# Softmax-minus-one-hot on one core: blocks of two rows per partition in three in-place f32 buffers, with a row maximum

## The chip, the core and the metric

The kernel runs on one core of a Trainium2 chip. The metric is the device time of one execution in microseconds (us). The chip's engines have short names: DVE is the vector engine, ACT the scalar engine, POOL the GpSimd engine, PE the tensor engine, SP the engine that here only issues loads. Sixteen DMA engines move data between HBM (the chip's main memory) and SBUF (the on-chip buffer of 128 partitions).

## The reference, cut to what matters

```python
batch, seq_len, vocab = 8, 1024, 8192            # 8192 rows of 8192 f32
logits_max = np.max(logits, axis=-1, keepdims=True)
exp_logits = np.exp(logits - logits_max)
softmax = exp_logits / np.sum(exp_logits, axis=-1, keepdims=True)
one_hot[batch_idx, seq_idx, labels] = 1.0
return (softmax - one_hot).astype(np.float32)
```

268.4 MB are read and 268.4 MB are written, whatever the kernel does. A tile of 128 rows is 4 MB; there are 64 of them. "Row" below means such a row of tiles: one matrix row on each of the 128 partitions.

## The kernel before

One tile per step, four f32 buffers, exp without a shift, a bf16 copy for the arithmetic, and one label transfer per tile:

```python
io_pool   = tc.tile_pool(name="io", bufs=4)            # f32, 128 x 8192
work_pool = tc.tile_pool(name="work", bufs=2)          # bf16
# ... cut: iota over the vocabulary, once
for ti in range(n_tiles):
    nc.sync.dma_start(out=logits_tile[:], in_=logits_nv[rs : rs + P, :])           # L47
    nc.gpsimd.dma_start(out=labels_tile[:], in_=labels_n[rs : rs + P, None])       # L50
    # ... cut: labels to f32
    nc.scalar.activation(out=exp_bf[:], in_=logits_tile[:], func=Exp,
                         bias=0.0, scale=1.0, accum_out=sum_f32[:])                # L61
    nc.vector.reciprocal(out=recip_sum[:], in_=sum_f32[:])
    nc.vector.tensor_scalar(out=ohts_bf, in0=iota_pv[:, :], scalar1=labels_f32[:],
                            scalar2=sum_f32[:], op0=is_equal, op1=mult)            # L74
    nc.vector.tensor_sub(out=exp_bf[:], in0=exp_bf[:], in1=ohts_bf)                # L83
    nc.vector.tensor_scalar_mul(out=logits_tile[:], in0=exp_bf[:],
                                scalar1=recip_sum[:])                              # L85
    nc.scalar.dma_start(out=out_nv[rs : rs + P, :], in_=logits_tile[:])            # L87
```

The softmax here doesn't subtract the row's maximum and nothing guards it: scores larger than these inputs give would overflow.

## Time and profile before

| | before |
|---|---|
| time, median of 3 runs | 1255.14 us |
| span of the profiled run | 1252.6 us |
| DVE, ACT busy | 58%, 36% |
| per tile, mid-run | 19.36 us |
| one 32 KB packet on its DMA engine | 1.213 us |
| idle of all DMA engines together | one stretch, 4.3 us, at the end |

The page of the kernel before starts with the span, the engines' busy time, the busy tenths of the DMA engines in 40 equal slices, and what they moved in each slice:

```profile
span 1252.6 us, 992 instructions
...
DVE 732.6 (58%) x320; ACT 457.0 (36%) x129; POOL 253.0 (20%) x69
...
DMA  9999999999999999999999999999999999999997
GB/s 400 421 435 434 433 428 430 433 436 433 435 430 432 431 433 433 434 434 432 429 432 435 431 434 433 431 432 432 434 433 434 433 429 432 432 434 435 434 433 311
```

The DMA engines are busy in every slice. Only the first two slices and the last move less than 425 GB/s. A transfer of 4 MB is 8 packets on each of 16 engines, so 128 transfers take 128 x 8 x 1.213 = 1242 us (the data packets of the trace add up to 1244 us per engine): nearly the whole span.

Next the costliest groups (line, engine, operation, operands, count | busy us, mean ns | idle before, and what ended it):

```profile
L61 ACT ACTIVATE exp_bf<-logits_tile 128x8192 bf16<-128x8192 f32 x64 | 449.8, 7029 | 771.3 <-DMA logits_tile<-in_logits_dram 757.8
...
L85 DVE TENSOR_SCALAR logits_tile<-exp_bf,recip_sum 128x8192 f32<-128x8192 bf16 x64 | 287.1, 4486 | 0.1
L83 DVE TENSOR_TENSOR exp_bf<-exp_bf,logits_tile 128x8192 bf16<-128x8192 bf16 x64 | 283.2, 4425 | 2.2
L74 DVE TENSOR_SCALAR logits_tile<-iota_pv,labels_f,sum_f 128x8192 bf16<-128x8192 int16 x64 | 154.3, 2412 | 0.3 <-issue 0.3
```

DVE's three passes cost 4.49 + 4.43 + 2.41 us per tile. The waits, of the compute engines and of the load queue (us in total, times, longest):

```profile
ACT exp_bf L61 <- DMA logits_tile<-in_logits_dram: 757.8, 62, 19.2
DVE recip_sum L71 <- ACT exp_bf L61: 485.1, 61, 10.5
```

```profile
SPq L47 <- DMA out_dram<-logits_tile: 1169.6, 60, 50.2
```

ACT waits for loads, and loads wait for stores to free a buffer. The loop is closed by the DMA engines. At the very end nothing is left to overlap with. The timeline of the last tile (start, duration, what, idle before it):

```profile
1221.87 7.03 ACT L61 ACTIVATE exp_bf<-logits_tile 128x8192 bf16<-128x8192 f32 x1 [12.24 <-DMA logits_tile<-in_logits_dram]
1221.92 0.34 ACTq L87 DMA_DIRECT2D out_dram<-logits_tile  x1
...
1229.11 2.41 DVE L74 TENSOR_SCALAR logits_tile<-iota_pv,labels_f,sum_f 128x8192 bf16<-128x8192 int16 x1
1231.56 4.43 DVE L83 TENSOR_TENSOR exp_bf<-exp_bf,logits_tile 128x8192 bf16<-128x8192 bf16 x1
1236.02 4.49 DVE L85 TENSOR_SCALAR logits_tile<-exp_bf,recip_sum 128x8192 f32<-128x8192 bf16 x1
1240.54 0.34 ACTq L87 DMA_DIRECT2D out_dram<-logits_tile  x1
```

The last load landed just before 1221.87, the last store left at 1240.54. The store before it left at 1221.92 and was done in between.

### The profile page before, as it was taken

The page shows a single profiled execution, that of the slowest core. Times are in us where ns is not written, and L with a number is a line of the kernel's source. Part 1 is how long each engine was busy: PE and PEld are TensorE (multiplying, and loading weights), DVE is VectorE, ACT ScalarE, POOL GpSimd, SP SyncE. Part 2 cuts the span into 40 slices and gives each one's busy share as a digit, 9 for nine tenths or more (in the row PEclk, how much of TensorE's full clock was granted, in tenths as well). Part 3 has the DMA queues.
Part 4 walks back from the last instruction along what each step waited for, and adds up shares of the span by engine and source line. Part 5 has one row for each costly group of instructions (what it writes and reads, how often), then busy time and mean ns, then how long its engine had stood idle before and what let it go on. Part 6 is the DMA issues. An engine that isn't in the chain of part 4 may idle for free.

```text
span 1252.6 us, 992 instructions
## 1 busy us (share of the span) xinstructions
DVE 732.6 (58%) x320; ACT 457.0 (36%) x129; POOL 253.0 (20%) x69
## 2 busy tenths in 40 slices
DVE  3764655746647556465574664755646556465573
ACT  4424244243342433423424334243342432423422
POOL 5322212212122122221221212212222122100000
DMA  9999999999999999999999999999999999999997
GB/s 400 421 435 434 433 428 430 433 436 433 435 430 432 431 433 433 434 434 432 429 432 435 431 434 433 431 432 432 434 433 434 433 429 432 432 434 435 434 433 311
DMA packets 20487, 537.01 MB, mean 429 GB/s; under 512 B 4096, under 2 KB 4096, under 8 KB 4096
## 3 DMA queue, kind: packets, MB, share of 16 engines
q1 hardware_dynamic: 9216, 268.44, 49.8%
q10 hardware_dynamic: 9216, 268.44, 49.6%
q0 software_dynamic: 2048, 0.07, 0.1%
q14 instruction: 7, 0.06, 0.0%
HBM read 268.50 MB, written 268.44 MB: 429 GB/s over the span
## 4 chain that ended last, share of the span: by engine, by line
DMA 71%; DVE 17%; issue 8%; ACT 1%; POOL 1%; ACTq 0%; SPq 0%; PEldq 0%
DMA out_dram<-logits_tile 38%; DMA logits_tile<-in_logits_dram 32%; DVE logits_tile L85 7%; DVE exp_bf L83 7%; DVE logits_tile L74 4%; ACT exp_bf L61 1%; DMA labels_tile<-in_labels_dram 1%; POOL iota_pv L41 1%; ACTq L87 0%; POOL labels_tile L50 0%; DVE labels_f L57 0%; DVE recip_sum L71 0%; SPq L47 0%; ACTq L61 0%; PEldq L113 0%
## 5 line engine op out<-in xcount | busy, mean ns | idle before, releaser
L61 ACT ACTIVATE exp_bf<-logits_tile 128x8192 bf16<-128x8192 f32 x64 | 449.8, 7029 | 771.3 <-DMA logits_tile<-in_logits_dram 757.8
L50 POOL DMA_DIRECT2D labels_tile<-in_labels_dram x64 | 245.9, 3843 | 832.1 <-DVE labels_f L57 830.1
L71 DVE RECIPROCAL recip_sum<-sum_f 128x1 f32<-128x1 f32 x64 | 10.5, 163 | 485.1 <-ACT exp_bf L61 485.1
L85 DVE TENSOR_SCALAR logits_tile<-exp_bf,recip_sum 128x8192 f32<-128x8192 bf16 x64 | 287.1, 4486 | 0.1
L83 DVE TENSOR_TENSOR exp_bf<-exp_bf,logits_tile 128x8192 bf16<-128x8192 bf16 x64 | 283.2, 4425 | 2.2
L74 DVE TENSOR_SCALAR logits_tile<-iota_pv,labels_f,sum_f 128x8192 bf16<-128x8192 int16 x64 | 154.3, 2412 | 0.3 <-issue 0.3
L57 DVE CAST labels_f<-labels_tile 128x1 f32<-128x1 int32 x64 | 9.4, 147 | 20.2 <-DMA labels_tile<-in_labels_dram 20.2
L61 ACT ACTIVATION_READ_ACCUMULATOR exp_bf<-logits_tile 128x1 f32 x64 | 11.9, 186 | 0.0
L41 POOL IOTA iota_pv<- 128x8192 int16 x1 | 6.9, 6944 | 0.4 <-PEq L113 0.4
L61 ACT ACT_TABLE_LOAD x1 | 1.3, 1283 | 0.7 <-PEq L102 0.7
L102 POOL MEMSET const-float32-0.0<- 128x1 f32 x1 | 0.1, 99 | 0.2 <-issue 0.2
L102 POOL MEMSET const-bfloat16-1.0<- 128x1 bf16 x1 | 0.1, 102 | 0.0
L102 POOL MEMSET const-uint8-127<- 128x1 uint8 x1 | 0.1, 102 | 0.0
L102 POOL MEMSET const-float32-1.0<- 128x1 f32 x1 | 0.1, 99 | 0.0
## 6 DMA issues: line engine op xcount, KB each, us to landing
logits_tile<-in_logits_dram SPq DMA_DIRECT2D x64, 4096.0 KB, 27.2
out_dram<-logits_tile ACTq DMA_DIRECT2D x64, 4096.0 KB, 31.3
labels_tile<-in_labels_dram POOLq DMA_DIRECT2D x64, 1.0 KB, 12.7
```

What stands on the lines that cost most here:

```text
L41: nc.gpsimd.iota(iota_pv[:, :], [[1, V]], channel_multiplier=0)
L50: nc.gpsimd.dma_start(out=labels_tile[:], in_=labels_n[rs : rs + P, None])
L57: nc.vector.tensor_copy(out=labels_f32[:], in_=labels_i32)
L61: nc.scalar.activation(out=exp_bf[:], in_=logits_tile[:], func=mybir.ActivationFunctionType.Exp, bias=0.0, scale=1.0, accum_out=sum_f32[:],)
L71: nc.vector.reciprocal(out=recip_sum[:], in_=sum_f32[:])
L74: nc.vector.tensor_scalar(out=ohts_bf, in0=iota_pv[:, :], scalar1=labels_f32[:], scalar2=sum_f32[:], op0=mybir.AluOpType.is_equal, op1=myb ...
L83: nc.vector.tensor_sub(out=exp_bf[:], in0=exp_bf[:], in1=ohts_bf)
L85: nc.vector.tensor_scalar_mul(out=logits_tile[:], in0=exp_bf[:], scalar1=recip_sum[:])
L102: nc = _bacc.Bacc("TRN2", target_bir_lowering=False, num_devices=1)
```

## The change

The change loads two adjacent rows per partition as one contiguous run of 64 KB, works in place in f32 (no bf16 copy), and so fits three buffers of two rows where there were four of one. It adds the row maximum that the reference has. It loads all labels once and lays them out with two small transposes. The scaling moves from DVE to ACT. The instruction order is written by hand. The core of the diff (set-up, label code, tile allocations and `store` cut; `store` issues one transfer per row, from ACT, for the blocks in `BY_ROW_OUT`):

```diff
-    io_pool = ctx.enter_context(tc.tile_pool(name="io", bufs=4))
-    work_pool = ctx.enter_context(tc.tile_pool(name="work", bufs=2))
+    # SLOTS = 3, G = 2, HALF = 4096, C = V // HALF; T = 64 rows, B = 32 blocks
+    x_b = x_nv.rearrange("(b p j) v -> b p j v", p=P, j=G)
+    io = ctx.enter_context(tc.tile_pool(name="io", bufs=SLOTS))   # [P, G, V] f32
+    ctx.enter_context(tc.manual_schedule())
...
+    def load(b):            # L74 by row, L76 as a block
+        if b in BY_ROW_IN:
+            for j in range(G):
+                nc.sync.dma_start(out=x[:, j, :], in_=x_b[b, :, j, :])
         else:
+            nc.sync.dma_start(out=x[:], in_=x_b[b])
+    def row_max(x):         # L81
+        nc.vector.tensor_reduce(out=m[:], in_=x[:], axis=X, op=Alu.max, negate=True)
+    def exponent(x, m):     # L86
+        nc.scalar.activation(out=x[:], in_=x[:], func=Act.Exp, bias=m[:], accum_out=s[:])
+    def normalize(x, r):    # L97, two halves
+        nc.scalar.activation(out=xc, in_=xc, func=Act.Copy, bias=0.0, scale=r[:])
+    def subtract(t, x):     # L102, two halves
+        nc.vector.scalar_tensor_tensor(out=xc, in0=iota[:], scalar=lab[...], in1=xc,
+            op0=Alu.is_equal, op1=Alu.subtract, reverse1=True)
...
+    BY_ROW_IN = (0, B - 1)
+    BY_ROW_OUT = range(B)
+    m = row_max(row(0))
+    for t in range(T):
+        s = exponent(row(t), m)
+        r = inverse(s)
+        if t + 1 < T:
+            m = row_max(row(t + 1))
+        if t > 0:
+            store(t - 1)
+        normalize(row(t), r)
+        subtract(t, row(t))
+    store(T - 1)
```

More of the change, by code (lines that the diff above doesn't have):

```diff
@@ L5 @@
 import concourse.tile as tile
-from concourse import bass_utils, mybir
+from concourse import mybir
 from concourse._compat import with_exitstack
 P = 128
+HALF = 4096
+SLOTS = 3
+G = 2
 @with_exitstack
@@ L21 @@
     fp32 = mybir.dt.float32
-    bf16 = mybir.dt.bfloat16
+    i32 = mybir.dt.int32
     i16 = mybir.dt.int16
-    logits_nv = logits.flatten_outer_dims()
-    out_nv = out.flatten_outer_dims()
-    labels_n = labels
-    while len(labels_n.shape) > 1:
-        labels_n = labels_n.rearrange("a b ... -> (a b) ...")
-    N, V = logits_nv.shape
-    assert N % P == 0, f"N={N} must be a multiple of {P}"
-    n_tiles = N // P
-    const_pool = ctx.enter_context(tc.tile_pool(name="const", bufs=1))
-    io_pool = ctx.enter_context(tc.tile_pool(name="io", bufs=4))
@@ L37 @@
-    work_pool = ctx.enter_context(tc.tile_pool(name="work", bufs=2))
-    stats_pool = ctx.enter_context(tc.tile_pool(name="stats", bufs=4))
-    iota_pv = const_pool.tile([P, V], i16)
-    nc.gpsimd.iota(iota_pv[:, :], [[1, V]], channel_multiplier=0)
-    for ti in range(n_tiles):
-        rs = ti * P
-        logits_tile = io_pool.tile([P, V], fp32, tag="io")
-        nc.sync.dma_start(out=logits_tile[:], in_=logits_nv[rs : rs + P, :])
-        labels_tile = stats_pool.tile([P, 1], labels_n.dtype, tag="labels")
-        nc.gpsimd.dma_start(out=labels_tile[:], in_=labels_n[rs : rs + P, None])
-        labels_f32 = stats_pool.tile([P, 1], fp32, tag="labels_f32")
-        if mybir.dt.size(labels_n.dtype) == 8:
-            labels_i32 = labels_tile.bitcast(mybir.dt.int32)[:, :1]
-        else:
-            labels_i32 = labels_tile[:]
-        nc.vector.tensor_copy(out=labels_f32[:], in_=labels_i32)
-        exp_bf = work_pool.tile([P, V], bf16, tag="exp")
-        sum_f32 = stats_pool.tile([P, 1], fp32, tag="sum")
-        nc.scalar.activation(
-            out=exp_bf[:],
-            in_=logits_tile[:],
-            func=mybir.ActivationFunctionType.Exp,
-            bias=0.0,
-            scale=1.0,
-            accum_out=sum_f32[:],
-        )
-        recip_sum = stats_pool.tile([P, 1], fp32, tag="recip")
-        nc.vector.reciprocal(out=recip_sum[:], in_=sum_f32[:])
-        ohts_bf = logits_tile.bitcast(bf16)[:, :V]
-        nc.vector.tensor_scalar(
-            out=ohts_bf,
-            in0=iota_pv[:, :],
-            scalar1=labels_f32[:],
-            scalar2=sum_f32[:],
-            op0=mybir.AluOpType.is_equal,
-            op1=mybir.AluOpType.mult,
-        )
-        nc.vector.tensor_sub(out=exp_bf[:], in0=exp_bf[:], in1=ohts_bf)
-        nc.vector.tensor_scalar_mul(out=logits_tile[:], in0=exp_bf[:], scalar1=recip_sum[:])
-        nc.scalar.dma_start(out=out_nv[rs : rs + P, :], in_=logits_tile[:])
@@ new lines @@
+    Act = mybir.ActivationFunctionType
+    Alu = mybir.AluOpType
+    x_nv = logits.flatten_outer_dims()
+    o_nv = out.flatten_outer_dims()
+    N, V = x_nv.shape
+    T = N // P
+    B = T // G
+    C = V // HALF
+    lab_bp = labels.rearrange("a b -> (a b)").rearrange("(b q) -> b q", q=G * P)
+    x_b = x_nv.rearrange("(b p j) v -> b p j v", p=P, j=G)
+    o_b = o_nv.rearrange("(b p j) v -> b p j v", p=P, j=G)
+    const = ctx.enter_context(tc.tile_pool(name="const", bufs=1))
+    io = ctx.enter_context(tc.tile_pool(name="io", bufs=SLOTS))
@@ new lines @@
+    stats = ctx.enter_context(tc.tile_pool(name="stats", bufs=4))
+    psum = ctx.enter_context(tc.tile_pool(name="psum", bufs=1, space=bass.MemoryType.PSUM))
+    ctx.enter_context(tc.manual_schedule())
+    lab_raw = const.tile([B, G * P], labels.dtype)
+    nc.scalar.dma_start(out=lab_raw[:], in_=lab_bp)
+    iota = const.tile([P, HALF], i16)
+    nc.gpsimd.iota(iota[:], [[1, HALF]], base=0, channel_multiplier=0)
+    ident = const.tile([B, B], fp32)
+    nc.gpsimd.memset(ident[:], 0.0)
+    nc.gpsimd.affine_select(
+        out=ident[:], in_=ident[:], compare_op=Alu.not_equal, fill=1.0,
+        base=0, pattern=[[-1, B]], channel_multiplier=1,
+    )
@@ new lines @@
+    lab_f = const.tile([B, G, P], fp32)
+    step = mybir.dt.size(labels.dtype) // 4
+    lab32 = lab_raw[:].bitcast(i32).rearrange("b (p j s) -> b j p s", j=G, s=step)
+    lab = const.tile([P, C, G, B], fp32)
+    lab_ps = psum.tile([P, G, B], fp32)
+    for j in range(G):
+        nc.vector.tensor_copy(out=lab_f[:, j, :], in_=lab32[:, j, :, 0])
+        nc.tensor.transpose(out=lab_ps[:, j, :], in_=lab_f[:, j, :], identity=ident[:])
+    for c in range(C):
+        nc.vector.tensor_scalar_add(out=lab[:, c], in0=lab_ps[:], scalar1=float(-c * HALF))
@@ new lines, in load @@
+    def load(b):
+        x = io.tile([P, G, V], fp32, tag="x", name="x")
+        if b in BY_ROW_IN:
+            for j in range(G):
+                nc.sync.dma_start(out=x[:, j, :], in_=x_b[b, :, j, :])
+        else:
+            nc.sync.dma_start(out=x[:], in_=x_b[b])
+        return x
+    def row_max(x):
+        m = stats.tile([P, 1], fp32, tag="m", name="m")
+        nc.vector.tensor_reduce(out=m[:], in_=x[:], axis=mybir.AxisListType.X, op=Alu.max, negate=True)
+        return m
+    def exponent(x, m):
+        s = stats.tile([P, 1], fp32, tag="s", name="s")
+        nc.scalar.activation(out=x[:], in_=x[:], func=Act.Exp, bias=m[:], scale=1.0, accum_out=s[:])
+        return s
@@ new lines, in inverse @@
+    def inverse(s):
+        r = stats.tile([P, 1], fp32, tag="r", name="r")
+        nc.vector.reciprocal(out=r[:], in_=s[:])
+        return r
+    def normalize(x, r):
+        for c in range(C):
+            xc = x[:, c * HALF : (c + 1) * HALF]
+            nc.scalar.activation(out=xc, in_=xc, func=Act.Copy, bias=0.0, scale=r[:])
+    def subtract(t, x):
+        for c in range(C):
+            xc = x[:, c * HALF : (c + 1) * HALF]
+            nc.vector.scalar_tensor_tensor(
+                out=xc, in0=iota[:], scalar=lab[:, c, t % G, t // G : t // G + 1], in1=xc,
+                op0=Alu.is_equal, op1=Alu.subtract, reverse1=True,
+            )
@@ new lines, in store, with row @@
+    def store(t):
+        b, j = divmod(t, G)
+        if b in BY_ROW_OUT:
+            nc.scalar.dma_start(out=o_b[b, :, j, :], in_=blocks[b][:, j, :])
+        elif j == G - 1:
+            nc.scalar.dma_start(out=o_b[b], in_=blocks[b][:])
+    BY_ROW_IN = (0, B - 1)
+    BY_ROW_OUT = range(B)
+    blocks = {}
+    def row(t):
+        b, j = divmod(t, G)
+        if b not in blocks:
+            blocks[b] = load(b)
+        return blocks[b][:, j, :]
+    m = row_max(row(0))
[8 more added lines that the diff above has]
+        subtract(t, row(t))
```

## The prediction

> **What bounds the kernel now.** The DMA engines. The page's slices show DMA at 9 tenths in 39 of 40; DVE is busy 58%, ACT 36%. In the trace a 32 KB packet takes 1.213 us on its engine, also when both queues are active. A 4 MB transfer is 8 packets on each of 16 engines; 128 transfers need 128 x 9.71 = 1243 us of the 1252.6 us span. The rest is about 3 us before the first packet, a slow first slice (400 GB/s), and an idle stretch of 5.5 us at the end, where the last tile is computed after its load landed. In the waits, exp waits 757.8 us for loads and the load queue 1169.6 us for stores: a free buffer starts a load. A tile takes 19.36 us.
>
> **What the change does, per tile (64 tiles).**
> - DVE loses the one-hot (2.41), the bf16 subtract (4.43) and the scaling (4.49). It gains a row maximum over 8192 f32 and two halves of compare-and-subtract, f32 with two tensor inputs. The Trainium skill, "VectorE: DVE Perf Modes", tier table, gives reductions and f32 two-input operations one element per cycle; the trace's bf16 subtract, 4.43 us for 8192, is the two-per-cycle form. I estimate 8.7 for the maximum and 2 x 4.43 for the halves: 17.7 us against 11.5 before, still under 19.36.
> - ACT gains a scaling of 2 x 3.6 us (estimate from the 7.03 us exp): 14.3 of 19.36.
> - The bytes stay. A block load in 64 KB packets saves one packet overhead in two: 1.213 us against an estimated 1.205 (a sixteenth of 435.2 GB/s, the skill's "DMA: Bandwidth & Descriptors", Where 436 GB/s comes from): 4 ns, some 2 us in all.
> - Buffering: six rows instead of four, but in blocks of two; a load needs both rows stored and lands as one. The next block's maximum precedes this block's last subtraction on DVE, so every second store waits for the next load plus 17.6 us. Load, compute and last store just fit the cycle of 3 x 38.7 = 116 us if the load queue gets two thirds of the engines (64 KB packets alternating with 32 KB ones). With equal shares some idle appears.
>
> **How much is on the critical path.** Almost none mid-run. My packet-by-packet tally of these durations gives 1252 us for the kernel before (measured 1252.6), and for the changed one 1258 with 64 KB packets, 1269 if they are split into 32 KB. The loss is at the ends: about 2 us near 70 us, and at the end, where the last two stores wait for the last maximum: about 10 us of idle DMA instead of 5.5.
>
> **Predicted time: 1260 us**, 8 in 10 between 1248 and 1274. Chances: faster by over 2% 0.02, within 2% 0.89, slower by over 2% 0.09.
>
> **What would show it.** DMA still 9 tenths in all middle slices; DVE about 90%, ACT about 73%; maximum near 8.7 us and each half near 4.4 us; load packets of 65536 bytes near 2.42 us; DVE waiting for a load every second row; last slice lower than 311 GB/s.
>
> **What would make it wrong.** A compare-and-subtract at two cycles per element would put DVE at 26 us per tile and the time near 1720. 64 KB packets cut in two, or equal sharing of the queues, cost some 10 us. Slower HBM access at the doubled pitch would show as packets over 1.213 us.

## The result, and the profile after

The changed kernel takes 1261.6 us (1260.77 to 1262.06, 4 runs) against 1254.86 us before (4 runs). The ratio is 1.0052, with a 95% interval of 1.0038 to 1.0067. Ratios here are the mean time of one kernel's runs over that of the other's of the same rounds, so they are not quite the ratio of the medians quoted. The difference of about 7 us is real but small.

The same lines of the page, now of the changed kernel:

```profile
span 1259.9 us, 830 instructions
...
PE 0.4 (0%) x2; PEld 0.3 (0%) x2; DVE 1120.4 (89%) x260; ACT 930.7 (74%) x257; POOL 4.0 (0%) x7
...
DMA  9999999999999999999999999999999999999996
GB/s 402 425 407 416 433 434 449 429 433 420 449 433 416 433 433 434 434 440 438 429 434 435 434 435 430 432 433 438 428 433 433 433 433 435 439 430 433 434 398 266
```

DVE went from 58% to 89% and ACT from 36% to 74%, yet the middle slices still move about 433 GB/s (single slices scatter from 407 to 449; over 600 to 700 us both kernels move 432). The difference stands mostly in the last two slices: 398 and 266 GB/s, where the kernel before had 433 and 311. The queues and the issues (the last number is the median us from issue to landing):

```profile
q10 hardware_dynamic: 9264, 268.51, 49.4%
q1 hardware_dynamic: 4896, 268.44, 49.4%
...
out_dram<-x ACTq DMA_DIRECT2D x64, 4096.0 KB, 27.4
...
x<-in_logits_dram SPq DMA_DIRECT2D x30, 33.1
```

q1, the loads, moved the same bytes in about half the packets. The trace has 3840 load packets of 65,536 bytes, with a median of 2.418 us, against 1.213 us for the 32 KB packets of the stores. So one packet of 64 KB saves 8 ns over two of 32 KB. The groups and the waits:

```profile
L81 DVE TENSOR_REDUCE m<-x 128x1 f32<-128x8192 f32 x64 | 555.3, 8677 | 108.2 <-DMA x<-in_logits_dram 108.2
L86 ACT ACTIVATE x<-x,m 128x8192 f32<-128x8192 f32 x64 | 455.8, 7122 | 174.4 <-DVE m L81 174.4
L102 DVE SCALAR_TENSOR_TENSOR x<-iota,lab,x 128x4096 f32<-128x4096 int16 x128 | 567.9, 4479 | 4.1 <-ACT x L97 4.1
L97 ACT ACTIVATE x<-x,r 128x4096 f32<-128x4096 f32 x128 | 467.7, 3700 | 123.8 <-DVE r L91 123.8
```

```profile
ACT x L86 <- DVE m L81: 174.4, 64, 7.4
...
DVE m L81 <- DMA x<-in_logits_dram: 108.2, 28, 4.8
```

```profile
SPq L76 <- DMA out_dram<-x: 1118.2, 28, 79.3
```

The load queue still waits for stores, as before. The maximum costs 8.68 us and each half of the compare-and-subtract 4.48 us. In the timeline, where one instruction starts about 0.1 us before the last has ended, a row takes DVE 17.4 us. DVE waits for a load 28 times, once in nearly every block. Those 108.2 us are real waits, but the DMA engines are busy in them and lose nothing. The end, in the timeline:

```profile
1217.24 8.67 DVE L81 TENSOR_REDUCE m<-x 128x1 f32<-128x8192 f32 x1
1217.29 0.34 ACTq L110 DMA_DIRECT2D out_dram<-x  x1
...
1225.83 8.87 DVE L102 SCALAR_TENSOR_TENSOR x<-iota,lab,x 128x4096 f32<-128x4096 int16 x2
...
1234.74 0.34 ACTq L110 DMA_DIRECT2D out_dram<-x  x1
1235.12 7.31 ACT L97 ACTIVATE x<-x,r 128x4096 f32<-128x4096 f32 x2 [1.96 <-DVE r L91]
1238.86 8.88 DVE L102 SCALAR_TENSOR_TENSOR x<-iota,lab,x 128x4096 f32<-128x4096 int16 x2 [4.09 <-ACT x L97]
1247.78 0.34 ACTq L110 DMA_DIRECT2D out_dram<-x  x1
```

Stores left at 1217.29, 1234.74 and 1247.78. The first two are 17.4 us apart, which is the pace of DVE. A store alone needs only 8 x 1.213 = 9.7 us of the engines. By the trace's packets all engines stood idle for 6.6 us and 3.2 us here, and for 1.1 us near 83 us, when the first block had just been stored.

The sum: idle stretches of 10.9 us instead of 4.3, that is 6.6 us more. The engines' packet time (all packet durations over 16) fell from 1246.7 to 1245.5, 1.2 us less. Together that is 5.4 of the 7.3 us by which the span grew. The other 2 us must be idle time of single engines, which this count of common stretches does not see: span less packet time grew by 8.6 us (5.8 to 14.4).

### The profile page after: what moved, and what is told of

The parts are those of the page before. It is cut to its first block, busy times and chain, and to the rows that moved or that the text cites. A ratio compares the mean times of both kernels' runs of the same rounds, so it can differ in the third digit from the quotient of the medians.

```text
span 1259.9 us, 830 instructions
## 1 busy us (share of the span) xinstructions
PE 0.4 (0%) x2; PEld 0.3 (0%) x2; DVE 1120.4 (89%) x260; ACT 930.7 (74%) x257; POOL 4.0 (0%) x7
## 4 chain that ended last, share of the span: by engine, by line
DMA 67%; DVE 28%; issue 2%; ACT 1%; DVEq 0%; SPq 0%; ACTq 0%
DMA x<-in_logits_dram 38%; DMA out_dram<-x 30%; DVE m L81 15%; DVE x L102 13%; ACT x L86 1%; DVEq L162 0%; ACT x L97 0%; DVE r L91 0%; SPq L76 0%; DVEq L81 0%; ACTq L110 0%; DVEq L102 0%
## 5 line engine op out<-in xcount | busy, mean ns | idle before, releaser
L81 DVE TENSOR_REDUCE m<-x 128x1 f32<-128x8192 f32 x64 | 555.3, 8677 | 108.2 <-DMA x<-in_logits_dram 108.2
L86 ACT ACTIVATE x<-x,m 128x8192 f32<-128x8192 f32 x64 | 455.8, 7122 | 174.4 <-DVE m L81 174.4
L102 DVE SCALAR_TENSOR_TENSOR x<-iota,lab,x 128x4096 f32<-128x4096 int16 x128 | 567.9, 4479 | 4.1 <-ACT x L97 4.1
L97 ACT ACTIVATE x<-x,r 128x4096 f32<-128x4096 f32 x128 | 467.7, 3700 | 123.8 <-DVE r L91 123.8
L91 DVE RECIPROCAL r<-s 128x1 f32<-128x1 f32 x64 | 10.1, 158 | 7.3 <-ACT x L86 7.3
L86 ACT ACTIVATION_READ_ACCUMULATOR x<-x,m 128x1 f32 x64 | 12.0, 187 | 0.0
L52 POOL IOTA iota<- 128x4096 int16 x1 | 3.5, 3541 | 0.4 <-POOLq L151 0.4
## 6 DMA issues: line engine op xcount, KB each, us to landing
out_dram<-x ACTq DMA_DIRECT2D x64, 4096.0 KB, 27.4
x<-in_logits_dram SPq DMA_DIRECT2D x30, 33.1
```

Source lines behind the costliest of these rows:

```text
L52: nc.gpsimd.iota(iota[:], [[1, HALF]], base=0, channel_multiplier=0)
L81: nc.vector.tensor_reduce(out=m[:], in_=x[:], axis=mybir.AxisListType.X, op=Alu.max, negate=True)
L86: nc.scalar.activation(out=x[:], in_=x[:], func=Act.Exp, bias=m[:], scale=1.0, accum_out=s[:])
L91: nc.vector.reciprocal(out=r[:], in_=s[:])
L97: nc.scalar.activation(out=xc, in_=xc, func=Act.Copy, bias=0.0, scale=r[:])
L102: nc.vector.scalar_tensor_tensor(out=xc, in0=iota[:], scalar=lab[:, c, t % G, t // G : t // G + 1], in1=xc, op0=Alu.is_equal, op1=Alu.subt ...
```

## The experiments

The theory, called A in the texts: mid-run the DMA engines set the pace, and the changed kernel loses time only where they run dry. That is mostly the end. The last block load lands early, DVE still has several rows to do at 17.4 us each, and each gives a store of only 9.7 us. How early DVE gets its rows, and how many stores are queued at the end, depends on when buffers come free and when loads land. The rivals put the loss in the middle of the run (packets, strided row stores, waits of DVE), or in the maximum as such.

The kernel before ran again beside every group of runs; its medians were 1254.86 to 1255.53 us, so runs of different groups can be compared to about 1 us.

"Tally" in these texts is my packet-by-packet reckoning: fixed durations read from the trace, the engines' instruction order, and two queues that alternate by packet. It is an estimate, and part of what the runs test. The tally gives spans; measured times lie about 2 us above.

The times are medians; the last two columns are counted in the profiled run. All outputs are right. Three of these lie some way from their median: e2_nomax (1250.96 us), e5_last2 (1259.88) and e10_joint (1286.27, where the six runs spread from 1285.9 to 1300.1).

| run | time, us | ratio to before | idle stretches, us | packets over usual, us |
|---|---|---|---|---|
| changed kernel | 1261.6 | 1.0052 | 10.9 | 4.2 |
| e1_pad32 | 1288.4 | 1.0259 | 17.1 | 24.7 |
| e2_nomax | 1248.2 | 0.9941 | none | 5.6 |
| e4_rowload | 1258.0 | 1.0018 | 5.1 | 5.9 |
| e5_last2 | 1258.0 | 1.0024 | 5.6 | 7.2 |
| g1_slots6 | 1248.3 | 0.9944 | none | 1.6 |
| e10_joint | 1289.6 | 1.0282 | 14.8 | 23.5 |
| e3_halfmax | 1251.7 | 0.9970 | 2.0 | 3.7 |
| e8_extra | 1432.2 | 1.1407 | 90.9 | 60.1 |
| e7_subfirst | 1864.0 | 1.4848 | 537.8 | 53.3 |
| e6_blockstore | 1377.9 | 1.0976 | 57.9 | 57.2 |
| g1_slots5 | 1258.4 | 1.0023 | 7.2 | 4.1 |
| g1_slots4 | 1324.2 | 1.0546 | 26.7 | 37.8 |

The fourth column adds all stretches of over 0.3 us in which no data packet was on any of the 16 engines, from the first packet on. The fifth adds what packets took beyond 1.213 us (32 KB) or 2.418 us (64 KB), over 16 engines.

### e1_pad32: the same load, but in 32 KB packets

```diff
-        x = io.tile([P, G, V], fp32, tag="x", name="x")
+        x = io.tile([P, G, V + 16], fp32, tag="x", name="x")[:, :, :V]
```

> Changed kernel (1261.6) with 16 unused elements after each row in the buffer, so that a block load has to move two 32 KB runs per partition instead of one of 64 KB; nothing else differs. Theory A (the two queues alternate packet by packet, so 64 KB load packets get two thirds of the engines; with equal shares loads arrive later, and more of the stores pile up behind the DVE at the end): about 1271 us, 16 load packets of 32768 bytes per engine, load landing longer than 33 us, stores quicker than 27 us, about 20 us of idle DMA instead of 14. Rival B (packet size matters only by its fixed few ns): 1263 to 1264.

Measured: 1288.4 us, 27 us over the changed kernel. Rival B falls. The direction is that of theory A, and so are the landings:

```profile
out_dram<-x ACTq DMA_DIRECT2D x64, 4096.0 KB, 21.4
x<-in_logits_dram SPq DMA_DIRECT2D x30, 8192.0 KB, 39.4
```

Compared with the changed kernel, a block load takes 39.4 instead of 33.1 us and a store 21.4 instead of 27.4. Packets of the two queues go in turn, so the queue with the bigger packets gets the bigger share: counted from the trace's packets where both queues have work (100 to 1180 us), loads hold 0.70 of the engines' time in the changed kernel, 0.48 in e1_pad32 and 0.50 in e4_rowload. The idle stretches came out near the expectation. But another 17 us were not foreseen: load packets averaged 1.248 us and store packets 1.226 us, where 1.213 is usual. They come throughout the run, not only at its start. See e10_joint and "What stays open".

### e2_nomax: no row maximum

```diff
-        nc.scalar.activation(..., func=Act.Exp, bias=m[:], ...)
+        nc.scalar.activation(..., func=Act.Exp, bias=0.0, ...)
-    m = row_max(row(0))            # and the call in the loop
```

> Changed kernel without the row maximum (exp with bias 0, as the kernel before has it; these inputs need no shift). Theory A (middle is at the DMA engines' pace with idle only at the ends, where the DVE's 17.4 us per row is slower than a 9.7 us store): the two idle stretches near the end vanish, about 1250 us, below the kernel before, DMA idle 4 to 5 us in all. Rival C (the extra 7 us are lost in the middle, to strided row stores or 64 KB packets): no gain beyond 2 us, about 1260.

Measured: 1248.2 us, no idle stretch left. The block loads, the strided row stores and the in-place f32 work are all still there, so none of them is the loss by itself: rival C falls. (Whether the coupling of two rows costs something only together with the maximum is tested by g1_slots6.) Without the maximum DVE has about 9 us of work per row left. This version has no shift in exp, as the kernel before has none.

### e4_rowload and e5_last2: rows that land one by one

```diff
-    BY_ROW_IN = (0, B - 1)
+    BY_ROW_IN = range(B)              # e4_rowload
+    BY_ROW_IN = (0, B - 2, B - 1)     # e5_last2
```

> Changed kernel with every block loaded row by row, so 32 KB packets and equal shares, but each row can be worked on as soon as it lands. Theory A: the earlier landing gives back what the equal shares cost, about 1259 us with the tally, 2 us under the changed kernel and about 12 us under e1_pad32, which has the same packets. Rival B (packet size and landing both without weight): 1263 to 1264, as e1_pad32.

> Changed kernel with the last two blocks loaded row by row instead of the last one only. Theory A (only the end loses time): the first idle stretch at the end shrinks from 6.6 us to about 2, total about 1258 us. Rival C (loss in the middle): 1261 to 1262, no change.

Measured: 1258.0 us both. For e4_rowload the same 32 KB packets that made e1_pad32 slow do no harm once each row may be worked on as it lands. For e5_last2 only the last two blocks differ, and the first idle stretch at the end shrank from 6.6 to 2.4 us, as theory A said. In its profiled run, which was only 1.9 us faster than the changed kernel's, packets ran 3 us longer in sum, most of it in the first 100 us; that takes up more than half of the 5.3 us of idle time saved.

### e10_joint: e4_rowload, but both rows of a block are awaited

```diff
+            if (t + 1) % G == 0 and 0 < (t + 1) // G < B - 1:
+                row(t + 1)
+                both_landed(blocks[(t + 1) // G])    # maximum of 8 elements of the second row
```

> As e4_rowload (every row its own 32 KB-packet load; 1258.0), but a tiny DVE instruction ahead of each block's first maximum makes it wait until both rows of the block have landed, as one block load would. Theory A (32 KB packets give equal shares, the joint landing makes that costly): about 1271 us, idle of about 20 us, packets at 1.213 us. Rival E (in e1_pad32 the slow packets, mean 1.248 us, came with 32 KB packets themselves and not with the two-run transfer): 1285 to 1290, as e1_pad32. Rival B (landing without weight): 1258.

Measured: 1289.6 us, 32 us over e4_rowload, for thirty tiny instructions. So the joint landing is what brings the loss, and rival B falls again. By the table about 10 us of it are idle stretches, as in theory A, and about 18 us are slow packets, which theory A does not have. Theory A's number was wrong by 19 us, in the same way as for e1_pad32: load packets averaged 1.246 us. As this kernel moves its rows in separate transfers, the two-run transfer is not what makes the slow packets. But e4_rowload has the same packets and next to none of them mid-run, so 32 KB packets by themselves are not the cause either, and rival E falls as I put it. The cause stays open (below).

### e3_halfmax and e8_extra: less and more work on DVE

```diff
-        nc.vector.tensor_reduce(out=m[:], in_=x[:], ...)
+        nc.vector.tensor_reduce(out=m[:], in_=x[:, :HALF], ...)      # e3_halfmax
```

```diff
+        nc.vector.tensor_reduce(out=m2[:], in_=x[:, :HALF], ...)     # e8_extra, beside the full one
```

> Changed kernel with the maximum taken over half a row only (still correct here, as any shift is): DVE 13.1 us per row instead of 17.4. Theory A: enough to catch up before the end, about 1249 us, like e2_nomax (1248.2). Rival F (what counts is that a maximum must precede exp at all, the added wait from landing to exp): little gain, 1256 to 1261.

> Changed kernel with a second maximum over half a row (4.4 us) on DVE per row: 21.8 us per row, above the 19.4 us that a row needs on the DMA engines. Theory A (DVE at 17.4 is hidden by 2 us per row only): the DVE becomes the bound, 1440 us by the tally, DVE over 95% busy. Rival: the DMA engines still cover most of it, under 1300.

Measured: 1251.7 and 1432.2 us. Half a maximum brings about three quarters of the gain of none (9.9 of 13.4 us; one stretch of 2.0 us is left), so it is the amount of DVE work that counts, not that exp has to wait for a maximum: rival F falls. Half a maximum more makes DVE the bound; the page of e8_extra (span, busy time, DVE's tenths):

```profile
span 1430.2 us, 893 instructions
...
PE 0.4 (0%) x2; PEld 0.3 (0%) x2; DVE 1394.4 (97%) x324; ACT 930.7 (65%) x257; POOL 4.0 (0%) x7
...
DVE  4999999999999999999999999999999999999995
```

A row's DVE work of 17.4 us is hidden under the 19.4 us of its transfers, with 2 us to spare. Another 4.4 us cost 170 us in all.

### e7_subfirst: DVE's order turned round

```diff
-        if t + 1 < T:
-            m = row_max(row(t + 1))
         if t > 0:
             store(t - 1)
         normalize(row(t), r)
         subtract(t, row(t))
+        if t + 1 < T:
+            m = row_max(row(t + 1))
```

> Changed kernel with DVE's order turned round: both halves of a row's subtraction ahead of the next row's maximum. Theory A (maximum, exp, scaling and subtraction of neighbouring rows overlap only because the next maximum runs while ACT scales; turned round they form one chain): about 1849 us by the tally, 28 to 29 us per row, DMA idle about a third. Rival G (order costs little, since DVE has 10% to spare and a store would even leave sooner): 1255 to 1275.

Measured: 1864.0 us. The work is the same, and rival G falls. One row in the timeline:

```profile
796.67 7.12 ACT L86 ACTIVATE x<-x,m 128x8192 f32<-128x8192 f32 x1 [13.95 <-DVE m L81]
...
804.12 7.31 ACT L97 ACTIVATE x<-x,r 128x4096 f32<-128x4096 f32 x2 [0.23 <-DVE r L91]
807.86 8.88 DVE L102 SCALAR_TENSOR_TENSOR x<-iota,lab,x 128x4096 f32<-128x4096 int16 x2 [3.77 <-ACT x L97]
816.66 8.68 DVE L81 TENSOR_REDUCE m<-x 128x1 f32<-128x8192 f32 x1
825.37 7.12 ACT L86 ACTIVATE x<-x,m 128x8192 f32<-128x8192 f32 x1 [13.94 <-DVE m L81]
```

Exp, scaling, subtraction and maximum stand one behind the other, 28.7 us from exp to exp (796.67 to 825.37). In the changed kernel the next row's maximum fills the time in which ACT scales, which is why it stands ahead of the subtraction, even though that holds back every second store.

### e6_blockstore: one store per block

```diff
-    BY_ROW_OUT = range(B)
+    BY_ROW_OUT = ()
```

> Changed kernel with one store per block instead of one per row, so that stores too move 64 KB packets. Theory A (the first row's early store is what keeps the engines fed while the second row is worked on; nothing is gained by bigger packets): about 1334 us by the tally, an idle stretch of 2 us in every block and DMA idle about 88 us in all. Rival H (bigger packets both ways save overhead): 1255 to 1262.

Measured: 1377.9 us. Rival H falls: the 64 KB store packets averaged 2.419 us, 7 ns less than two of 32 KB, some 2 us over the run, and the late store costs far more. Without the early store of the first row the engines run dry in every block. The tally had put 88 us of idle and no slow packets; measured were 57.9 us in stretches common to all engines and 57.2 us of slow packets. The size of the loss was too low by 44 us.

### g1_slots6, g1_slots5, g1_slots4: buffers of one row

```diff
-SLOTS = 3
-G = 2
+SLOTS = 6        # 5 and 4 in the other two
+G = 1
```

> Changed kernel with one row per partition in a block and six buffers: the same bytes of buffer and the same work on every engine (maximum kept), but a row's buffer is free when that row is stored, and a row is worked on when that row lands. Theory A (coupling two rows in one buffer makes loads start late and leaves the DVE behind at the end): tally 1250 us of span, 1251 to 1253 us measured, DMA idle 2 to 4 us, no idle stretch near the end; faster than the kernel before. Rival D (the maximum's 8.7 us on DVE by itself makes the tail, whatever the buffers): about 1260 with idle stretches of 6.6 and 3.2 us as in the changed kernel.

> As g1_slots6 (1248.3) with five buffers of one row instead of six. Theory A (the sixth row of buffer is what lets DVE run ahead and covers the end): tally 1257 of span, 1258 to 1259 measured, idle stretches near the end of 1.4 and 2.8 us, little idle in the middle. Rival I (not the number of rows but the coupling in twos was the loss): 1248 to 1250.

> As g1_slots6 with four buffers of one row, as many as the kernel before has. Theory A: tally 1282 of span, 1284 measured, idle mostly near the end, with a tenth of it early. A second thing to see: whether the load queue now runs empty between loads, and whether then packets over the usual 1.213 us come in the middle of the run as in e1_pad32 and e10_joint (mean 1.246 us and more); if restarts of the load queue make them, the time is 1290 to 1310. Rival I: 1250 to 1255.

Measured: 1248.3, 1258.4 and 1324.2 us. With six buffers of one row, the same bytes of buffer and the maximum kept, no idle stretch is left, the time is even 3 us under the expected range, and the kernel beats both the kernel before and the changed one: ratio to before 0.9944, interval 0.9932 to 0.9956 (real, though "same" by the 2% rule). Rival D falls. This kernel also moves its loads in 32 KB packets; e4_rowload does so too, with two rows still freed together, and takes 1258.0 us. So of the 13.3 us between the changed kernel and this one, about 3.6 come with the landing row by row and 9.7 with the release row by row. The page (span, DMA tenths, GB/s) and the issues of g1_slots6:

```profile
span 1246.2 us, 997 instructions
...
DMA  9999999999999999999999999999999999999998
GB/s 405 421 438 433 429 434 436 432 432 433 435 432 430 435 434 433 429 435 435 431 430 434 438 429 431 435 436 428 432 436 435 429 432 435 436 430 430 436 435 379
```

```profile
x<-in_logits_dram SPq DMA_DIRECT2D x64, 4096.0 KB, 24.2
out_dram<-x ACTq DMA_DIRECT2D x64, 4096.0 KB, 54.9
```

A store now takes 54.9 us from issue to landing, not 27.4. At one store per 19.4 us, almost three stores are in the queue on average: DVE has run ahead, and the work has piled up where it does good. The end shows it:

```profile
1197.57 0.34 ACTq L110 DMA_DIRECT2D out_dram<-x  x1
...
1208.04 8.87 DVE L102 SCALAR_TENSOR_TENSOR x<-iota,lab,x 128x4096 f32<-128x4096 int16 x2
...
1216.94 0.34 ACTq L110 DMA_DIRECT2D out_dram<-x  x1
...
1221.07 8.88 DVE L102 SCALAR_TENSOR_TENSOR x<-iota,lab,x 128x4096 f32<-128x4096 int16 x2 [4.08 <-ACT x L97]
1229.98 0.34 ACTq L110 DMA_DIRECT2D out_dram<-x  x1
```

The stores again leave 19.4 and 13.0 us apart, slower than they are carried out, but the queue still holds earlier ones, and the last two slices move 435 and 379 GB/s.

Five buffers lose that lead (1258.4 us), within the expected range, and so rival I falls: it is both, the release row by row and the number of rows. Four lose far more than the tally's 1284 us, with 37.8 us of slow packets. The load queue does run empty there and slow packets do come with it, as the expectation put it (the store queue runs empty too, see below), but the time of 1324.2 us lies over its range too.

### What stays open

In six runs (e1_pad32, e10_joint, e6_blockstore, e7_subfirst, e8_extra, g1_slots4) packets beyond the usual time come all through the run, 19 to 51 us in sum between 100 and 1180 us. In the other runs and the two kernels it is at most 1.2 us in that stretch. An empty load queue is not what sets them apart: in the changed kernel, too, the load queue stands empty for about 11 us in nearly every block, without slow packets. The store queue does. In these six runs it stands empty for over 3 us 25 to 38 times in that stretch of the run, 147 to 695 us in all; in the other eight kernels at most 7 times, 30 us in all. In each of the six, half or more (52 to 99%) of the extra time is in packets that overlap such a gap of the store queue. This is a coincidence in time, read from the traces afterwards; no run tested it, and why packets take longer there was not found.

## Why the prediction was right

- **The bound stays with the DMA engines: right.** The middle slices read 9 tenths before and after; e8_extra shows that the margin is 2 us per row.
- **The costs: right.** Estimated 8.7 us for the maximum and 4.43 for a half, measured 8.68 and 4.48. ACT was put at about 73% and is at 74%, DVE at about 90% and is at 89%. DVE waits for a load 28 times, as foreseen for every second row. The Trainium skill, "VectorE: DVE Perf Modes", tier table, has reductions and f32 two-input operations at one element per cycle; the trace agrees for the reduction: 8192 f32 elements in 8.68 us, twice the 4.43 us of the bf16 subtract, which the table has at two per cycle. The compare-and-subtract, with a scalar and two tensors, is not in the table; its 4096 elements in 4.48 us go at the rate of the reduction.
- **64 KB packets: right, in size as well.** 2.418 against 2 x 1.213 us, 8 ns per 64 KB, some 2 us over 3840 packets on 16 engines (3840 / 16 x 0.008). The prediction's 1.205 us for 32 KB without overhead came from the fabric rate in the Trainium skill, "DMA: Bandwidth & Descriptors", section "Where 436 GB/s comes from"; the saving agrees with it.
- **The queues' shares: right.** The loads' landing of 33.1 us became 39.4 when e1_pad32 halved their packets. The Trainium skill, "DMA: Bandwidth & Descriptors", section "Queues, rings and completion order", has each engine take packets from its queues in turn; the trace doesn't name a packet's engine, but where both queues have work loads hold 0.70 of the engines' time in the changed kernel, and packets in turn would give 2.418 of 3.631, or 0.67.
- **The loss is at the ends: right.** The last slice fell from 311 to 266 GB/s. Predicted was about 10 us of idle at the end; measured were 6.6 + 3.2. The early one was put at 2 us near 70 us and was 1.1 us near 83. The end of the kernel before was put at 5.5 us; counted over all engines together it is 4.3.
- **The time:** 1260 predicted, 1261.6 measured.
- **The side remark that was wrong in size:** "64 KB packets cut in two, or equal sharing of the queues, cost some 10 us". e1_pad32 did just that and cost 27 us. The idle part was as reckoned. The mis-sized term is the packet itself, which the tally kept at 1.213 us and which averaged 1.248 (loads) and 1.226 us (stores). The tally has no term for slow packets, and it missed e1_pad32, e10_joint, e6_blockstore and g1_slots4, which have them, by 17 to 44 us. That the changed kernel has next to none was not foreseen; to that extent the closeness of the 1260 us is luck.
- **The step that the prediction did not see:** it took the loss at the end as the price of the maximum. g1_slots6 shows it is the price of the maximum with buffers that are freed two rows at a time: with six single rows and the same maximum no idle stretch is left.

## What to carry to other kernels

When the DMA engines are the bound, as here, compute up to the transfer time of a tile is free mid-run but not at the end: look there for the pace at which the last stores leave. Free and refill buffers in the smallest piece that still moves at full rate; larger packets gained 8 ns per 64 KB here, and the coupling of two rows lost 13 us. Keep enough such pieces: the sixth buffer of one row was worth 10 us. A store queue with several entries waiting is a good sign, since it is what the engines live on when the loads have ended.

## What the Trainium skill lacked or had wrong

- "DMA: Bandwidth & Descriptors", section "Rules for kernel authors", has at least 1 MiB per DMA for full bandwidth. Another section has the engines change queues at packet boundaries, but the page does not draw the conclusion that bigger packets take a bigger share. Here a load queue with 64 KB packets beside a store queue with 32 KB ones landed 8 MB in 33.1 us, and in 39.4 us with 32 KB packets.
- "HBM Reference", section "Specifications (TRN2)", has about 425 GB/s for a core streaming alone. Mid-run both kernels held 432 GB/s (600 to 700 us), with loads and stores together.
- No page has the packets that take longer than usual all through a run, which came here in the runs whose store queue runs empty mid-run (in e1_pad32 means of 1.248 and 1.226 us against 1.213, some 20 us in all).
- "VectorE: DVE Perf Modes", tier table, has no row for the operation with a scalar and two tensors. With an int16 and an f32 input and f32 output it took 4.48 us for 4096 elements, about the rate of the f32 maximum (8192 in 8.68 us). The remark on this operation in "Vector Engine (DVE) Microarchitecture Reference", section "7. Points that are easy to get wrong", gives no time.
